# Copying 96 rows of the last batch from HBM to HBM, by index registers on the SyncE queue, with the other stores moved to ScalarE's queue

## The chip, the cores and the metric

One Trainium2 chip, one core. The time is device microseconds of the kernel; medians of a few executions are quoted. Some executions are slow (here: more than 1.5% above the fastest of the same kernel). The medians take them in; a ratio does not: it is the mean time of one kernel's fast runs over that of the other's of the same rounds, so it is not quite the ratio of the quoted medians.

## The reference

```python
def setup_inputs():
    batch, seq, dim = 32, 512, 1024
    return {
        "x": np.random.randn(batch, seq, dim).astype(np.float32),
        "indices": np.random.randint(0, seq, (batch, 128)).astype(np.int32),
    }

def reference(x, indices):
    for b in range(32):
        result[b] = x[b, indices[b]]      # 128 rows of 4 KB for each batch
```

## The kernel before

The first five batches (`HEAD`) are gathered by index into SBUF (the on-chip memory of 128 partitions) and stored. Every other batch has some repeated indices. TensorE and VectorE compute which rows are distinct, GpSimd gathers only those (a slot without a row gets an index out of bounds and is skipped) into one of eight buffers `u`, and a matmul with a 0/1 matrix spreads them to their places; ScalarE copies the result from PSUM (the memory that TensorE writes) and SyncE issues the store. Batch 5 takes part of its rows from two early loads of 128 rows. The slots that stay empty move round all 128 partitions, so that all DMA engines get the same number of rows.

```python
    rank = const.tile([N, 8, 16], I32, name="rank")     # slot number of each partition, for each of 8 groups
    ...
    def store(b):
        if b not in PAIRED:
            nc.sync.dma_start(out=of[b * N:(b + 1) * N], in_=blocks[b])
        elif b % 2:
            nc.sync.dma_start(out=..., in_=blocks[b - 1, "pair"][:])   # two batches in one

    for b in range(HEAD):
        gather(blocks[b], first[:]... if b == 0 else idxT[:, b:b + 1], b)
        store(b)
    ...
    for b in range(HEAD, B):
        spread_rows(b)          # 2 x (matmul, ScalarE copy), then store(b)
        fetch(b + RING)         # the next gather into the buffer that came free
        ...                     # one step of the index work of a later group
```

Of the kernel before, what the change touches and what calls it, by code (L numbers as in the profile page):

```python
# [6 lines left out]
F32 = mybir.dt.float32  # L7
F16 = mybir.dt.float16
I32 = mybir.dt.int32
ALU = mybir.AluOpType  # L10
# [18 lines left out]
def kernel(ctx, tc, x, indices, out):  # L29
# [11 lines left out]



    nc = tc.nc
    B, S, D = x.shape
    N = indices.shape[1]
    HEAD, RING, GROUP, AHEAD, FAR = 5, 8, 3, 4, 1024
    HALF = HEAD
    PAIRED = range(12, 20)
    GROUPS = (B - HEAD) // GROUP  # L50
    assert 2 * N <= S <= FAR and (B - HEAD) % GROUP == 0
    const = ctx.enter_context(tc.tile_pool(name="const", bufs=1))
    ring = ctx.enter_context(tc.tile_pool(name="ring", bufs=1))
    rows = ctx.enter_context(tc.tile_pool(name="rows", bufs=1))
    pick = ctx.enter_context(tc.tile_pool(name="pick", bufs=1))
    junkp = ctx.enter_context(tc.tile_pool(name="junk", bufs=4))
    PS = bass.MemoryType.PSUM
    pbc = ctx.enter_context(tc.tile_pool(name="pbc", bufs=2, space=PS))
    psm = ctx.enter_context(tc.tile_pool(name="psm", bufs=1, space=PS))
    pout = ctx.enter_context(tc.tile_pool(name="pout", bufs=4, space=PS))  # L60
    pe, dve, act = InOrder(tc), InOrder(tc), InOrder(tc)
    mm, v = nc.tensor.matmul, nc.vector
# [4 lines left out]
    vals = const.tile([B, N], indices.dtype, name="vals")  # L67
# [2 lines left out]

    diff = const.tile([N, N], I32, name="diff")
    nc.gpsimd.iota(diff[:], pattern=[[1, N]], base=0, channel_multiplier=-1)
    rank = const.tile([N, 8, 16], I32, name="rank")
    for e in range(8):
        fold = 0
        for bit, col in enumerate((6, 5, 3)):
            fold ^= col * (e >> bit & 1)
        steps = [[(-16 if fold >> bit & 1 else 16) << bit, 2] for bit in (2, 1, 0)]
        nc.gpsimd.iota(rank[:, e], pattern=[[1, 2]] + steps, base=2 * e + 16 * fold, channel_multiplier=0)
    less = const.tile([N, 1], F32, name="less")  # L80
    zero = const.tile([N, 1], F32, name="zero")
    dve(v.memset, zero[:], 0.0)
# [4 lines left out]
    above = const.tile([N, N], F16, name="above")  # L87
    dve(v.tensor_scalar, out=above[:], in0=diff[:], scalar1=0, scalar2=None, op0=ALU.is_gt)
    dve(v.tensor_copy, out=less[:], in_=diff[:, 0:1])
    every = const.tile([N, N], F16, name="every")  # L90
    dve(v.memset, every[:], 1.0)
    turn = const.tile([N, N], F16, name="turn")
    dve(v.tensor_copy, out=turn[:], in_=rank[:].rearrange("p e q -> p (e q)"))
    vf = const.tile([N, N], F16, name="vf")
    dve(v.memset, vf[:], 0.0)
    dve(v.tensor_copy, out=vf[:B],
        in_=vals[:].bitcast(I32).rearrange("p (n two) -> p n two", two=2)[:, :, 0])
# [4 lines left out]
    for k in range(2):  # L102
        load = act(nc.scalar.dma_start, out=early[k][:], in_=xf[HALF * S + k * N:HALF * S + (k + 1) * N])
        if k == 0:
# [7 lines left out]
    idxT = const.tile([N, B], I32, name="idxT")  # L112
# [3 lines left out]
    near = const.tile([N, B], F16, name="near")  # L116
    dve(v.tensor_scalar, out=near[:], in0=tr[:], scalar1=float(-FAR), scalar2=None, op0=ALU.add)

    of = out.flatten_outer_dims()

    def gather(dst, at, b, **kw):
        nc.gpsimd.indirect_dma_start(  # L122
            out=dst, out_offset=None,
            in_=xf[:], in_offset=bass.IndirectOffsetOnAxis(ap=at, axis=0),
            element_offset=b * S * D, **kw)


    blocks = {}
    for b in range(B):
        if b not in PAIRED:  # L130
            blocks[b] = rows.tile([N, D], F32, name=f"block{b}")[:]
# [3 lines left out]
            blocks[b, "pair"] = pair  # L135

    def store(b):
        if b not in PAIRED:
            nc.sync.dma_start(out=of[b * N:(b + 1) * N], in_=blocks[b])
        elif b % 2:  # L140
            nc.sync.dma_start(out=of[(b - 1) * N:(b + 1) * N].rearrange("(t p) d -> p t d", t=2),
                              in_=blocks[b - 1, "pair"][:])

    for b in range(HEAD):
        gather(blocks[b], first[:].bitcast(I32)[:, 0:1] if b == 0 else idxT[:, b:b + 1], b)
        store(b)

    def table(name, dtype):
        return const.tile([N, B], dtype, name=name)

    cnt, lead, slot = table("cnt", F32), table("lead", F16), table("slot", F16)
    nth, at = table("nth", I32), table("at", I32)
    past = const.tile([N, B + 1], F16, name="past")
    dve(v.memset, past[:, HEAD:HEAD + 1], 0.0)
    bcs, packs, spread = {}, {}, {}

    def of_group(g):
        return range(HEAD + g * GROUP, HEAD + (g + 1) * GROUP)

    def cols(t, g):  # L160
        return t[:, HEAD + g * GROUP:HEAD + (g + 1) * GROUP]

    def wide(t):
        return t.rearrange("p (g o) -> p g o", o=1).to_broadcast([N, GROUP, N])

    def step0(g):

# [3 lines left out]
        for k, b in enumerate(of_group(g)):  # L171
            junk = junkp.tile([N, N], F16, name="junk")
            dve(v.scalar_tensor_tensor, out=junk[:], in0=bc[:, k], scalar=idxF[:, b:b + 1], in1=below[:],
                op0=ALU.is_equal, op1=ALU.mult, accum_out=cnt[:, b:b + 1])
        if HALF in of_group(g):
            c = slice(HALF, HALF + 1)
            dve(v.scalar_tensor_tensor, out=cnt[:, c], in0=idxF[:, c], scalar=2.0 * N, in1=cnt[:, c],
# [4 lines left out]

    def step1(g):

        rk = psm.tile([N, GROUP], F32, name="rk")
        pe(mm, rk[:], lhsT=above[:], rhs=cols(lead, g), start=True, stop=False)
        pe(mm, rk[:], lhsT=every[:], rhs=cols(past, g), start=False, stop=True)
        dve(v.tensor_copy, out=cols(nth, g), in_=rk[:])
        dve(v.tensor_scalar, out=cols(nth, g), in0=cols(nth, g), scalar1=N - 1, scalar2=None, op0=ALU.bitwise_and)
        dve(v.scalar_tensor_tensor, out=cols(slot, g), in0=cols(cnt, g), scalar=256.0, in1=cols(nth, g),  # L190
            op0=ALU.mult, op1=ALU.add)
        packs[g] = pack = junkp.tile([N, GROUP, N], F16, name="pack")
        dve(v.tensor_tensor, out=pack[:], in0=turn[:].rearrange("p (o n) -> p o n", o=1).to_broadcast([N, GROUP, N]),
            in1=wide(cols(slot, g)), op=ALU.is_equal)

    def step2(g):

        pos = psm.tile([N, GROUP], F32, name="pos")
        for k, b in enumerate(of_group(g)):
            pe(mm, pos[:, k:k + 1], lhsT=packs[g][:, k], rhs=near[:, b:b + 1], start=True, stop=True)  # L200
        dve(v.tensor_scalar, out=cols(at, g), in0=pos[:], scalar1=float(FAR), scalar2=None, op0=ALU.add)
        s = pick.tile([N, GROUP, N], F32, name=f"s{g}")
        dve(v.tensor_tensor, out=s[:], in0=bcs[g][:, :GROUP], in1=wide(cols(at, g)), op=ALU.is_equal)
        for k, b in enumerate(of_group(g)):
            spread[b] = s[:, k]

    def fetch(b):
        if HEAD <= b < B:
            gather(held[(b - HEAD) % RING][:], at[:, b:b + 1], b, bounds_check=S - 1, oob_is_err=False)

    held = []
# [5 lines left out]
    def half_spread():  # L217

        same = pick.tile([N, 2, N], F32, name="same")
        for k in range(2):  # L220
            dve(v.tensor_scalar, out=same[:, k], in0=bcs[0][:, HALF - HEAD], scalar1=less[:], scalar2=float(k * N),
                op0=ALU.add, op1=ALU.is_equal)
        spread[HALF, "early"] = [same[:, k] for k in range(2)]

    def half_rows(h, last):
        w = slice(h * 512, (h + 1) * 512)
        if not last:
            spread[HALF, h] = pout.tile([N, 512], F32, name="ps")
        ps = spread[HALF, h]
        if last:  # L230
            pe(mm, ps[:], lhsT=spread[HALF], rhs=held[(HALF - HEAD) % RING][:, w], start=False, stop=True)
        else:
            for k in range(2):
                pe(mm, ps[:], lhsT=spread[HALF, "early"][k], rhs=early[k][:, w], start=k == 0, stop=False)
        if last:
            nc.scalar.copy(out=blocks[HALF][:, w], in_=ps[:])  # L236

    def spread_rows(b):
        for h in range(2):
            if b == HALF:  # L240
                half_rows(h, True)
                continue
            w = slice(h * 512, (h + 1) * 512)
            ps = pout.tile([N, 512], F32, name="ps")
            pe(mm, ps[:], lhsT=spread[b], rhs=held[(b - HEAD) % RING][:, w], start=True, stop=True)
            nc.scalar.copy(out=blocks[b][:, w], in_=ps[:])  # L246
        store(b)

    step0(0)
    step0(1)  # L250
    for g in range(AHEAD):
        step1(g)
        if 0 < g < AHEAD - 1:
            step0(g + 1)
        step2(g)
        for b in of_group(g):
            if b < HEAD + RING:
                fetch(b)
        if g == 0:
            half_spread()  # L260
        elif g < 3:
            half_rows(g - 1, False)
    for b in range(HEAD, B):
        spread_rows(b)
        fetch(b + RING)
        g, step = divmod(b - HEAD, GROUP)
        if g + AHEAD < GROUPS:
            (step0, step1, step2)[step](g + AHEAD)
# [30 lines left out]
```

## Time and profile before

| | before |
|---|---|
| time, median of 4 | 88.56 us (87.42 to 88.88) |
| span of the profiled run | 85.4 us |
| DMA | 32.91 MB, 406 GB/s of HBM traffic over the span |
| busy: TensorE, ScalarE, GpSimd, VectorE | 72%, 48%, 40%, 37% |

The span is what the profiler saw from the first to the last instruction; the time of the same execution is 1.8 us longer (87.19 us). The DMA row of the page (busy tenths of the 16 engines, in 40 slices) is the row to read here: it is full from start to end. The prediction below shows these lines and reads them.

### The profile page before, as it was taken

What the parts mean: (1) busy time and instruction counts of PE and PEld (TensorE: products, weight loads), DVE (VectorE), ACT (ScalarE), POOL (GpSimd) and SP (SyncE); (2) the same over time, 40 slices, a digit from 0 to 9 for tenths busy, and PEclk for the clock granted to TensorE, in tenths of its full rate; (3) what the DMA queues carried; (4) which work ended last, traced back from release to release, by engine and by line L of the source; (5) the groups of instructions that cost most, each with busy time, mean ns of one, the idle gap of its engine ahead of it and who ended that gap; (6) DMA issues with size and microseconds to landing.
All of it is one profiled execution on the core that took longest, in us unless ns stands there. A gap on an engine that the chain in (4) does not pass through costs nothing.

```text
span 85.4 us, 829 instructions
## 1 busy us (share of the span) xinstructions
PE 61.1 (72%) x189; PEld 25.5 (30%) x189; DVE 31.7 (37%) x160; ACT 40.6 (48%) x63; POOL 33.9 (40%) x45
## 2 busy tenths in 40 slices
PE   0310379460999999999999999997879988884000
PEld 0300142220434444354444444442212333320000
DVE  3698892864318547375485473000000000000000
ACT  0999920000145566656655666675553454445000
POOL 7687777837024554444555544466000000000000
PEclk9999999999569999999999999999999999999655
DMA  0999999999999999999999999999999999999990
GB/s 1 319 401 263 259 405 413 417 413 426 416 416 424 411 420 420 413 428 418 411 424 416 411 418 418 416 424 418 413 424 418 413 428 413 418 424 418 414 372 23
DMA packets 9636, 32.91 MB, mean 385 GB/s; under 512 B 1584, under 2 KB 1616, under 8 KB 9632
## 3 DMA queue, kind: packets, MB, share of 16 engines
q1 hardware_dynamic: 4736, 16.81, 48.3%
q0 software_dynamic: 4608, 15.01, 45.0%
q10 hardware_dynamic: 288, 1.05, 3.4%
q8 instruction: 1, 0.02, 0.1%
q14 instruction: 3, 0.02, 0.1%
HBM read 17.86 MB, written 16.78 MB: 406 GB/s over the span
## 4 chain that ended last, share of the span: by engine, by line
PE 39%; DMA 21%; DVE 11%; issue 8%; POOL 7%; another core or an unknown queue 2%; ACT 1%; POOLq 1%; SPq 0%; DVEq 0%
PE ps L24 36%; DMA u<-in_x_dram,at 20%; POOL u L122 7%; DVE junk L24 3%; DMA vals<-in_indices_dram 2%; DVE past L24 2%; PE bc L24 2%; DVE pack L24 1%; DVE s L24 1%; DVE nth L24 1%; PE pos L24 1%; DVE lead L24 1%; ACT block L246 1%; DVE same L24 1%
## 5 line engine op out<-in xcount | busy, mean ns | idle before, releaser
L24 PE MATMUL ps<-u,s 128*128 128x512 f32 x108 | 52.8, 624 | 3.4 <-DMA u<-in_x_dram,at 3.4
L122 POOL DMA_INDIRECT u<-in_x_dram,at x27 | 26.9, 998 | 23.8 <-PE ps L24 7.2
L246 ACT COPY block<-ps 128x512 f32<-128x512 f32 x36 | 21.1, 586 | 16.5 <-PE ps L24 15.4
L24 PEld LDWEIGHTS ps<-u,s 128*128 128x128 f32 x108 | 18.9, 193 | 24.7 <-issue 13.4
L246 ACT COPY pair<-ps 128x512 f32<-128x512 f32 x16 | 9.4, 586 | 5.8 <-PE ps L24 4.2
L24 DVE SCALAR_TENSOR_TENSOR junk<-bc,idxF,below 128x128 f16<-128x128 f32 x27 | 8.0, 347 | 7.9 <-PE bc L24 7.9
L24 ACT COPY u<-zero 128x1024 f32<-128x1024 f32 x8 | 7.7, 1040 | 0.0
L236 ACT COPY block<-ps 128x512 f32<-128x512 f32 x2 | 1.2, 586 | 13.2 <-PE ps L24 13.2
L24 PE MATMUL pos<-near,pack 128*128 128x1 f16 x27 | 2.0, 167 | 7.4 <-DVE nth L24 2.9
L24 PE MATMUL ps<-early,same 128*128 128x512 f32 x8 | 5.7, 855 | 0.0
L24 DVE TENSOR_TENSOR pack<-turn,slot 128x384 f16<-128x384 f16 x9 | 5.0, 558 | 0.3
L24 DVE TENSOR_TENSOR s<-bc,at 128x384 f32<-128x384 f32 x9 | 5.0, 557 | 0.3
L24 PEld LDWEIGHTS <-pack 128*128 128x128 f16 x27 | 1.7, 99 | 11.2 <-DVE pack L24 4.3
L24 DVE TENSOR_TENSOR past<-past,lead 128x1 f16<-128x1 f16 x27 | 4.4, 163 | 0.9
L122 POOL DMA_INDIRECT block<-in_x_dram,idxT x4 | 4.1, 1036 | 1.2 <-issue 0.9
L24 PE MATMUL bc<-vf,ident 128*128 128x128 f16 x27 | 3.5, 257 | 1.3 <-DVE same L24 1.3
L24 PEld LDWEIGHTS <-ident 128*128 128x128 f16 x27 | 2.5, 114 | 4.9 <-issue 4.9
L24 DVE TENSOR_SCALAR at<-pos 128x3 int32<-128x3 f32 x9 | 1.4, 160 | 4.2 <-PE pos L24 3.5
L24 DVE CAST nth<-rk 128x3 int32<-128x3 f32 x9 | 1.4, 159 | 4.0 <-PE rk L24 1.9
L21 PE MATMUL pos<-ident,vf 128*128 128x32 f16 x1 | 0.2, 208 | 3.2 <-DVE vf L24 3.2
L24 PE MATMUL rk<-lead,above 128*128 128x3 f16 x9 | 1.6, 172 | 1.1 <-DVE lead L24 1.1
L24 ACT ACT_TABLE_LOAD x1 | 1.3, 1283 | 2.2 <-DVE ident L24 2.2
(31 smaller groups left out, 18.4 us busy)
## 6 DMA issues: line engine op xcount, KB each, us to landing
out_dram<-block SPq DMA_DIRECT2D x24, 512.0 KB
out_dram<-pair SPq DMA_DIRECT2D x4, 1024.0 KB
early<-in_x_dram ACTq DMA_DIRECT2D x2, 512.0 KB
u<-in_x_dram,at POOLq DMA_INDIRECT x27
block<-in_x_dram,idxT POOLq DMA_INDIRECT x4
vals<-in_indices_dram SPq DMA_DIRECT2D x1, 32.0 KB
first<-in_indices_dram SPq DMA_DIRECT2D x1, 1.0 KB
block<-in_x_dram,first POOLq DMA_INDIRECT x1
```

What stands on the lines that cost most here:

```text
L21: self.last = do(*args, **kw)
L24: self.last = do(*args, **kw)
L122: nc.gpsimd.indirect_dma_start(out=dst, out_offset=None, in_=xf[:], in_offset=bass.IndirectOffsetOnAxis(ap=at, axis=0), element_offset=b * ...
L236: nc.scalar.copy(out=blocks[HALF][:, w], in_=ps[:])
L246: nc.scalar.copy(out=blocks[b][:, w], in_=ps[:])
```

## The change

The intent is to save DMA work. A row that goes through SBUF passes the DMA engines twice (gather and store); a row that is copied from HBM to HBM passes once. So 96 of the 128 rows of batch 31 are copied directly. A direct copy takes its row number from a register, eight of which are loaded at a time from an SBUF table, and is cut so that two DMA engines share it. To keep the engines level, five slots of the gather are left empty in most batches, and 123 go round instead of 128. SyncE now issues the row copies, three after each batch, and ScalarE the stores of the spread batches.

The diff, cut to its core (the arithmetic of the slots has more lines):

```diff
+    LONE = B - 1
+    BEGIN = 32
+    MAIN = N - 5
-    rank = const.tile([N, 8, 16], I32, name="rank")     (eight iotas)
+    rank = const.tile([N, 2, 64], I32, name="rank")
+    nc.gpsimd.iota(rank[:], pattern=[[56, 2], [2, 8], [1, 2], [14, 4]], base=-2, channel_multiplier=0)
+    nc.gpsimd.iota(rank[:, :, :8], pattern=[[8, 2], [1, 2], [2, 4]], base=112, channel_multiplier=0)
...
     def store(b):
+        queue = nc.sync.dma_start if b < HEAD else nc.scalar.dma_start
...
+    def halves(row):
+        return row.rearrange("o (a b d) -> (o b) a d", a=2, b=2)
+    def go_alone():
+        for n in range(BEGIN, N, LOAD):
+            loads += nc.values_load_multi_w_load_instructions(flat[LONE:LONE + 1, n:n + LOAD], engines=[SP], ...)[1]
+            for row in loads:
+                nc.sync.dma_start(out=halves(out[LONE, n:n + 1]), in_=halves(x[LONE][bass.ds(row, 1)]))
+                yield
...
+    gather(blocks[LONE][:BEGIN], idxT[:BEGIN, LONE:LONE + 1], LONE)
+    nc.sync.dma_start(out=of[LONE * N:LONE * N + BEGIN], in_=blocks[LONE][:BEGIN])
+    rows_alone(18)
...
         store(b)
+        rows_alone(3)
```

## The prediction

> **What bounds the kernel now.** I read the page's slices of the span first.
>
> ```profile
> span 85.4 us, 829 instructions
> PE   0310379460999999999999999997879988884000
> DMA  0999999999999999999999999999999999999990
> GB/s 1 319 401 263 259 405 413 417 413 426 416 416 424 411 420 420 413 428 418 411 424 416 411 418 418 416 424 418 413 424 418 413 428 413 418 424 418 414 372 23
> DMA packets 9636, 32.91 MB, mean 385 GB/s; under 512 B 1584, under 2 KB 1616, under 8 KB 9632
> ```
>
> The 16 DMA engines are busy in every slice but the first and the last, while TensorE starts late and ends early. Packets under 8 KB less those under 2 KB are 9632 - 1616 = 8016 rows of 4 KB: 4096 stored, 256 of the early load, and 3664 gathered (640 for the first five batches, 3024 for the other 27, whose repeated indices are skipped). The table of stretches shows how firm this bound is.
>
> ```profile
> 5.00:10.00 5.00, 0.62 (x7) 0.34 (x7) 4.29 (x23) 5.00 (x6) 3.62 (x5) 1.00 0.99 300
> 30.00:40.00 10.00, 10.00 (x35) 4.37 (x34) 5.96 (x30) 6.34 (x11) 5.13 (x6) 1.00 1.03 419
> 70.00:75.00 5.00, 4.21 (x10) 1.35 (x8) 0.00 (x0) 2.65 (x5) 0.00 (x0) 1.00 1.03 419
> 80.00:85.40 5.40, 0.00 (x0) 0.00 (x0) 0.00 (x0) 0.00 (x0) 0.00 (x0) 0.50 0.59 242
> ```
>
> The last columns are DMA share and GB/s. From 15 to 80 us the rate stays near 419, so one engine moves 26.2 GB/s, and a row of 4096 bytes costs 156 ns of one engine. 8016 rows / 16 engines = 501 rows, 78.2 us: nearly the span. The end of the chain of waits says the same: a transfer, the last matmuls and copies, and then the stores still queued.
>
> ```profile
> 58.96 16.67 DMA u<-in_x_dram,at
> 75.77 1.97 PE ps L24 x4
> 77.76 0.59 ACT block L246
> ```
>
> So compute matters only where it leaves DMA without work, and a DMA that can be issued only after the others are done adds its full time. For the cost of issuing I read the tile view of the output, and what SyncE waits for.
>
> ```profile
> L139 SPq DMA_DIRECT2D out_dram<-block x24: 332/332/360, 7.2 to 78.4; - x24
> L141 SPq DMA_DIRECT2D out_dram<-pair x4: 372/374/387, 40.9 to 52.3; - x4
> SPq L139 <- ACT block L246: 30.1, 18, 2.1
> ```
>
> One issue takes 0.33 to 0.37 us of the sequencer; today SyncE has only 30 and waits for ScalarE's copies.
>
> **What the Trainium skill says.** All from its page "DMA: Bandwidth & Descriptors".
> - "Why a DMA increments its semaphore by 16 and not by 1": the slowest dimension of the access patterns sets how many engines take part, and from SyncE and ScalarE these are the lowest-numbered. An outer dimension of two means engines 0 and 1. The trace before has no such DMA and cannot confirm it.
> - "The descriptor swizzle": in a transfer of 128 partitions, partitions 64 to 71 belong to engines 8 and 9. The new ranks leave just partitions 66, 67 and 69 to 71 mostly empty. If that table holds for the indirect gather, the wrong pair is relieved. The profile has no engine numbers, so this is open.
> - "Latency and other measured facts": a register load (tensor_load) costs at least some 600 ns. The trace before has none.
> - [...]the index load issues at 1.19 us and its data is used at 2.94, in the timeline.
>
> **The change, part by part.**
>
> *DMA volume.* Batch 31 was gathered (113 distinct rows) and stored (128): 241 row passes. Now 32 + 32 pass through SBUF and 96 go from HBM to HBM once: 160. Saved 81 passes / 16 x 156 ns = 0.8 us, if all engines stay equal. This is the whole intended gain, 0.9%.
>
> *Balance.* The 96 rows are 48 on each of two engines, 48 x 156 ns = 7.5 us if a 1 KB piece costs a quarter of a row. I worked the slots out from the fixed draw: two engines get 144 and 120 gathered rows over the 26 spread batches, the others about 188. If those two are the ones that copy, they carry 192 and 168 and all is level. If they are not, each copying engine carries 48 rows too many.
>
> *Head.* In the order of the built program the second small iota now stands behind the first gather on GpSimd, and the cast of the rank table, which needs it, stands in VectorE's fixed order ahead of the indices' transpose. Before:
>
> ```profile
> 2.34 0.23 DVE L24 CAST turn<-rank 128x128 f16<-128x128 int32 x1 [0.59 <-POOL rank L79]
> 2.76 1.12 POOL L122 DMA_INDIRECT block<-in_x_dram,first  x1 [0.45 <-DMA first<-in_indices_dram]
> 4.18 0.95 POOL L122 DMA_INDIRECT block<-in_x_dram,idxT  x1 [0.30 <-DVE past L24]
> ```
>
> The cast moves from 2.34 to about 4.2 us (gather ends at 3.88, then an iota of about 0.2). Cast, vf, transpose, idxT took about 1.0 us of work, so the second gather goes at 5.3 instead of 4.18: 1.1 us later. DMA is not at full rate there anyway (300 GB/s from 5 to 10 us), and the first store fills some of the hole; I book 0.5 us.
>
> *VectorE and TensorE.* Four more small VectorE operations per group, 4 x 9 x 0.17 = 6 us on an engine busy 37%, and nine more tiny matmuls: beside DMA, nothing.
>
> *Stores on ScalarE.* 22 issues of about 0.35 us, some 8 us beside its 40.6 busy: hidden by itself. But DMA completions of SyncE and ScalarE share eight semaphores in rotation, and each DMA waits until the last user of its semaphore is done. Reading semaphore numbers and wait values in the built program, some stores now wait for the store two batches back (blocks 7, 8, 11, 24, 25), where eight could be out before. That may leave some holes; I book 1 us.
>
> *The row copies at the end: the part that decides.* The same listing shows SyncE's rows falling behind. In the semaphores' order the store of batch 30, the last, comes ahead of row copy 74 (counting from 0), and that copy waits for it. SyncE issues in order, so row copies 74 to 95, 22 of 96, cannot start before the last big store has landed. They then run with nothing beside them: 22 x (0.33 us issue + about 0.12 for the address arithmetic in registers and the wait, my estimate) = 9.9 us, and the two register loads in that stretch (eight indices each) at 0.6 to 1.6 us, say 1.1, give 2.2. Sum 12.1 us, paced by SyncE, not by the two engines: one row is two 1 KB pieces each, about 80 ns.
>
> *Sum.* DMA now ends about 84.2 us into the span. The last store: 84.2 - 0.8 + 0.5 (head) + 1.0 (waits) = 84.9 if the relieved engines are the right ones. If not, engines 0 and 1 carry 37 of the 74 copied rows without relief, 37 - 5 saved = 32 rows x 156 ns = 5 us later than before, about 89.5. I can't tell which and take 87. Plus 0.5 for the semaphore to reach SyncE, 12.1 for the tail, 1.5 for the last copy to land, 1.2 from last packet to span end: 102.3. The measured median is about 2 to 3 us over the span (88.36 against 85.4), which would give 104.8. I shade it to 102, because a DMA to two engines may issue faster than one to sixteen.
>
> **The rivals.**
> 1. *All hidden, small gain.* Row copies run beside the big transfers, SyncE is ahead, engines level: 0.8 us less, minus the head, 87.5 to 88.5. For it: the care in the slot numbers, and SyncE's idleness now. Against it: the wait of row copy 74 on the last store, a wait on a constant that cannot be overtaken.
> 2. *Wrong engines, no tail.* The waits cost little but engines 0 and 1 carry 48 extra rows: 7.5 us less some 1 us saved, about 94 to 95. For it: the swizzle in the skill; against: someone chose partitions 64 to 71 and five slots, presumably with a reason.
> 3. *SyncE slower than I think.* If register addresses make an issue 0.8 us, the tail is 22 x 0.8 + 3 = 21 us, and the time 108 to 112. Nothing in the trace before speaks to it.
> 4. *Throttled stores.* ScalarE stuck behind semaphores holds PSUM and so TensorE: DMA share falls under 0.9 in the middle, 3 to 5 us on top of any of these.
>
> **Range and chances.** The tail is certain by the order of the program, and even at 0.33 us a row with 0.6 us loads it is 8.5 us: with the last store at 81 at best, 81 + 8.5 + 3 + 2 = 94.5. The bottom of the range, 93, is a little under that; the top, 111, is the slow issue with the wrong engines in part. Faster by 2% would need under 86.6, more than the full saving: 3%. Within 2%: 6%, if I misread the semaphores. Slower: 91%.
>
> **What would show it.** Right: the DMA row of the page falls to about one tenth in the last five or six slices, with a few tens of GB/s; the chain of waits ends in SyncE issues of the row copies; the last ScalarE copy is some 15 us before the end. The second gather starts near 5.3 us. The 0.45 us step between row copies is read from SyncE's timeline near the end. Engines level: the DMA share stays 1.0 until the last store; wrong pair: a shelf at two tenths of activity ahead of the tail. Wrong: row copies finished while stores still run, and full DMA up to the end.

## The result, and the profile after

The changed kernel takes 129.07 us (127.71 to 129.41, 4 runs). The ratio to before is 1.466, 95% interval 1.443 to 1.488: far slower, and 18 us above the top of the range.

The page of the kernel after, by slices:

```profile
span 127.2 us, 1164 instructions
PE   0212756698989729999956679595000000000000
ACT  1996000155336043465304163643400000000000
DMA  2989999999999999979999997474552000000000
GB/s 29 344 276 280 392 384 416 415 414 412 398 411 406 420 388 401 350 202 415 342 407 410 403 396 307 199 321 171 215 207 88 5 3 5 4 5 5 4 4 4
```

A slice is 3.18 us here. The kernel has three stretches: DMA nearly full to slice 24 (76 us), though with holes that the kernel before has not; half full to slice 30 (97 us); and a tail of nine slices with 3 to 5 GB/s. The table of stretches (columns as in the prediction: last are DMA share and GB/s) gives the last two in numbers:

```profile
70.00:80.00 10.00, 7.76 (x16) 2.71 (x16) 0.00 (x0) 3.75 (x8) 0.09 (x1) 1.00 0.87 352
80.00:90.00 10.00, 6.54 (x14) 2.49 (x14) 0.00 (x0) 4.30 (x8) 0.00 (x0) 1.00 0.54 218
90.00:100.00 10.00, 0.00 (x0) 0.00 (x0) 0.00 (x0) 1.58 (x3) 0.00 (x0) 0.50 0.41 162
100.00:110.00 10.00, 0.00 (x0) 0.00 (x0) 0.00 (x0) 0.00 (x0) 0.00 (x0) 0.50 0.02 5
```

(The lower mean clock of this run, 0.83, comes mostly from the tail: it reads 0.50 from 90 us on, where TensorE has nothing to do. It does not set the end, which is SyncE's.)

What runs in the tail, from SyncE's timeline near the end (start, length, what), and what one such issue costs, from the tile view of the output and the view of the line that loads the registers (min/median/max in ns, first and last start):

```profile
95.60 29.29 SPq L165 DMA_DIRECT2D out_dram<-in_x_dram  x31
```

```profile
L165 SPq DMA_DIRECT2D out_dram<-in_x_dram x96: 7/632/978, 9.7 to 124.3; - x96
L146 ACTq DMA_DIRECT2D out_dram<-block x18: 338/339/353, 26.2 to 93.9; - x18
L148 ACTq DMA_DIRECT2D out_dram<-pair x4: 378/383/389, 47.7 to 66.6; - x4
```

```profile
L159 SPq TENSOR_LOAD <-flat x12: 15/1058/2494, 8.7 to 117.1; - x12
```

The issue of a row copy takes 0.63 us where the issue of a store of 128 rows takes 0.34. With the address arithmetic, a register move and the gaps between them the step from one row copy to the next is 0.84 us, and each group of eight adds a load of 1.06 us. Thus 96 x 0.84 + 12 x 1.06 = 93 us: SyncE alone, never waiting, needs more than the whole span of before, and its first copy goes out at 9.7 us. In the tail it does not wait for anything: 31 copies in 29.29 us, with three loads between them, and 31 x 0.84 + 3 x 1.06 is 29.2. Earlier it does wait, for stores; from its list of waits (us in total, times, longest):

```profile
SPq L165 <- DMA out_dram<-block: 7.0, 2, 5.4
SPq L165 <- DMA out_dram<-pair: 4.2, 3, 2.5
```

That is 11.2 us more on SyncE.

The last store is issued at 93.9 us, where before it was at 78.4. What held it is in the list of waits of ScalarE (us in total, times, longest):

```profile
ACT block L295 <- DMA out_dram<-in_x_dram: 13.8, 6, 4.6
ACT block L295 <- DMA out_dram<-block: 6.4, 3, 2.7
ACT pair L295 <- DMA out_dram<-block: 5.8, 1, 5.8
```

26 us of waits for DMAs. In the kernel before ScalarE never waits for a DMA, as it issues no stores. A semaphore is a counter that a DMA raises when its data has landed. The DMAs of SyncE and ScalarE take their completion semaphores in turn from the same eight, and each is issued only when the previous user of its semaphore is done. In the built program's listing the store of batch 30, for instance, comes after row copy 61 on its semaphore, that one after the store of batch 25 (in the trace they go out in this order, at 93.9, 91.0 and 81.4 us). So stores wait for row copies that SyncE has not reached yet, and ScalarE stops copying. TensorE's weight loads then wait 21.8 us for ScalarE's copies (11.2 before), and GpSimd's gathers 11.7 us for TensorE (7.2 before).

The head came as predicted. From the timeline of the kernel after:

```profile
3.94 0.19 POOL L82 IOTA rank<- 128x16 int32 x1
4.16 0.23 DVE L24 CAST turn<-rank 128x128 f16<-128x128 int32 x1 [2.14 <-POOL rank L82]
5.47 0.95 POOL L128 DMA_INDIRECT block<-in_x_dram,idxT  x1 [1.35 <-DVE idxF L24]
```

The second gather starts at 5.47 us; it was 4.18.

### The profile page after: what moved, and what is told of

Same layout as the page of the kernel before. It is cut to its first block, busy times and chain, and to the rows that moved or that the text cites. A ratio compares the mean times of both kernels' runs of the same rounds, so it can differ in the third digit from the quotient of the medians.

```text
span 127.2 us, 1164 instructions
## 1 busy us (share of the span) xinstructions
PE 61.9 (49%) x192; PEld 24.8 (20%) x192; DVE 36.5 (29%) x194; ACT 37.5 (29%) x61; POOL 33.2 (26%) x39
## 3 DMA queue, kind: packets, MB, share of 16 engines
q1 hardware_dynamic: 1536, 3.18, 6.8%
## 4 chain that ended last, share of the span: by engine, by line
DMA 28%; SPq 11%; PE 10%; issue 9%; DVE 8%; ACT 3%; ACTq 1%; POOL 1%
DMA out_dram<-pair 13%; PE ps L24 8%; SPq L165 7%; DMA out_dram<-in_x_dram 7%; DMA out_dram<-block 6%; SPq L159 4%; ACT block L295 2%; DVE turns L24 2%; DVE nth L24 2%; DMA first<-in_indices_dram 1%; ACTq L146 1%; DVE junk L24 1%; ACT pair L295 1%; PE pos L24 1%; DVE pack L24 1%
## 5 line engine op out<-in xcount | busy, mean ns | idle before, releaser
L128 POOL DMA_INDIRECT u<-in_x_dram,at x26 | 26.3, 1013 | 32.4 <-PE ps L24 11.7
L295 ACT COPY block<-ps 128x512 f32<-128x512 f32 x34 | 18.3, 588 | 25.6 <-DMA out_dram<-in_x_dram 13.8
L295 ACT COPY pair<-ps 128x512 f32<-128x512 f32 x16 | 9.1, 589 | 12.6 <-DMA out_dram<-block 5.8
L128 POOL DMA_INDIRECT block<-in_x_dram,idxT x5 | 4.6, 924 | 2.6 <-DVE idxF L24 1.3
L285 ACT COPY block<-ps 128x512 f32<-128x512 f32 x2 | 1.2, 586 | 13.5 <-issue 13.5
L24 DVE TENSOR_TENSOR pack<-turn,slot 128x384 f16<-128x384 f16 (+1 forms) x9 | 4.9, 544 | 0.3
L24 DVE TENSOR_TENSOR s<-bc,at 128x384 f32<-128x384 f32 (+1 forms) x9 | 4.9, 543 | 0.3
L24 PEld LDWEIGHTS <-above 128*128 128x128 f16 x18 | 1.9, 111 | 6.4 <-issue 6.4
L24 DVE TENSOR_SCALAR turns<-rk 128x3 f32<-128x3 f32 (+1 forms) x9 | 1.4, 159 | 3.7 <-PE rk L24 3.6
L24 PE MATMUL rk<-lead,above 128*128 128x3 f16 (+1 forms) x18 | 1.8, 169 | 1.0 <-DVE cnt L24 1.0
L24 PEld LDWEIGHTS ps<-early,same 128*128 128x128 f32 x8 | 1.9, 257 | 1.5 <-issue 1.5
```

Of the source, the lines that this page charges most:

```text
L24: self.last = do(*args, **kw)
L128: nc.gpsimd.indirect_dma_start(out=dst, out_offset=None, in_=xf[:], in_offset=bass.IndirectOffsetOnAxis(ap=at, axis=0), element_offset=b * ...
L285: nc.scalar.copy(out=blocks[HALF][:, w], in_=ps[:])
L295: nc.scalar.copy(out=blocks[b][:, w], in_=ps[:])
```

## The experiments

The theories that the runs were to tell apart: A, SyncE's issue of the row copies is simply too long for one queue; B, row copies and stores wait for each other through the shared semaphores; C, the wrong pair of DMA engines was relieved; D, the stores cost where they are now. Kernels with a wrong result by intent are marked.

**1. No row copies.** The whole of batch 31 is gathered and stored early; everything else stays.

```diff
-    BEGIN = 32
-    MAIN = N - 5
+    BEGIN = N
+    MAIN = N
-    alone = go_alone()
+    alone = iter(())
```

> Theory A (SyncE's issue of 96 row copies, about 0.84 us each plus 1.05 us per load of eight indices, is the longest queue) and theory B (row copies and big stores wait for each other through eight shared semaphores) both say that without row copies the kernel is bound by its DMA volume again: 88 to 90 us, a little over the kernel before for the later second gather. A rival D, that the stores on the ScalarE queue cost by themselves, would leave it at 93 us or more.

89.96 us, ratio 1.019 (1.012 to 1.027). So the row copies bring nearly all of the loss. (Its result was wrong: with an even number of slots in rotation the rounding points, by my reading of the formula, one row in 256 at a slot that does not exist. Run 8 uses 127 slots and is correct.)

**2. Half of the row copies.**

```diff
-    BEGIN = 32
-    MAIN = N - 5
+    BEGIN = 80
+    MAIN = N - 2
```

> 48 row copies. Theory A: SyncE needs 8.3 + 48 x 0.84 + 6 x 1.1 + 2.5, plus some waits, about 60 to 65 us, and is done before the stores are: 88 to 91 us. Theory B alone: stores still stand behind row copies up to the middle, so 95 us or more. Theory C (the wrong pair of DMA engines is relieved): about 2.5 us on top of A, 91 to 93.

92.54 us, correct, ratio 1.049 (1.042 to 1.056). The last row copy is issued at 74 us, so SyncE is not the end here, and still 3% are lost against run 1. ScalarE waits 11.5 us in four waits for row copies. Halving the rows takes away 37 of the 41 us, far more than half: above some number of rows SyncE's queue outlasts the stores, and below it the rest is left: the waits, the head (run 8) and perhaps the wrong pair. The time lies in the range that the expectation gave for theory C; this run does not part it from the waits.

**3. Fixed addresses (wrong result).** The source row is a constant; no loads, no address arithmetic.

```diff
-            loads += nc.values_load_multi_w_load_instructions(...)[1]
+            loads = [None] * LOAD
...
-                nc.sync.dma_start(out=halves(out[LONE, n:n + 1]), in_=halves(x[LONE][bass.ds(row, 1)]))
+                nc.sync.dma_start(out=halves(out[LONE, n:n + 1]), in_=halves(x[LONE, n:n + 1]))
```

> Wrong result on purpose: the 96 rows are copied from fixed addresses, without loads of indices and address arithmetic. Theory A with the register address as the cost: an issue falls from 0.63 us to 0.33 to 0.40 us, a row from 0.84 to about 0.45, SyncE is done by about 60 us, and the time is 88 to 95 (the top if theory C holds too). If a small DMA on two engines costs 0.63 us whatever its address, SyncE needs 8 + 96 x 0.7 = 75 us and the time is 90 to 105.

101.91 us (2 runs), ratio 1.158 (1.149 to 1.168). The tile view of the output in this run, and below that in run 4:

```profile
L163 SPq DMA_DIRECT2D out_dram<-in_x_dram x96: 606/626/1457, 1.7 to 94.5; - x96
```

The issue still takes 0.63 us: the register is not what makes it dear. It costs the rest of the step (0.84 against 0.68 us) and the loads. As the first copies go out at 1.7 us instead of 9.7, and 96 x 0.68 are 65 us, this kernel shows what remains when SyncE's work is shorter than the span: it still loses 14 us. Two things are seen in its trace. ScalarE waits 21.1 us for row copies and stores before its copies, and between 90 and 94 us the DMA share is 0.37. And the early loads, now behind row copies, go out at 4.6 and 8.7 us (1.7 and 2.1 in the change), so that the second slice has 27 GB/s where the change has 344. How the 14 us divide, between these and the wrong pair (run 9), was not tested.

**4. Fixed addresses, 16 engines (wrong result).** As run 3, each row in 16 pieces of 256 bytes.

```diff
-        return row.rearrange("o (a b d) -> (o b) a d", a=2, b=2)
+        return row.rearrange("o (b d) -> (o b) d", b=16)
```

> Wrong result on purpose: e_fixed_rows with each row in 16 pieces of 256 bytes on 16 engines instead of four of 1 KB on two. If the 0.63 us of an issue come from using fewer than 16 engines, the issue falls to 0.33 to 0.40 us. If they come from the HBM to HBM form, it stays near 0.63 us. The time: relief no longer fits, but no engine is overloaded: 90 to 102, the top if the issue stays.

```profile
L163 SPq DMA_DIRECT2D out_dram<-in_x_dram x96: 509/587/1723, 1.6 to 85.4; - x96
```

Issue 0.59 us: nor is it the number of engines. The DMAs from HBM to HBM in these runs, of 2 or 16 engines, with registers or without, took 0.59 to 0.64 us to issue in the median (the one long copy of run 7: 0.78). Those between HBM and SBUF from SyncE and ScalarE took 0.33 to 0.46 in the median, but for SyncE's first five stores in run 4 (0.52); single ones go up to 1.1. Why is open. The time, 111.05 us (2 runs, the profiled one slow; the fast one 109.92), fell outside what I expected; the scheduler had put 20 of the copies ahead of the first store, and I did not follow it further.

**5. Stores on the GpSimd queue.** Its semaphores are others, so after row copy 17 no row copy waits for a store and no store for a row copy.

```diff
-        queue = nc.sync.dma_start if b < HEAD else nc.scalar.dma_start
+        queue = nc.sync.dma_start if b < HEAD else nc.gpsimd.dma_start
```

> The stores of the spread batches go on the GpSimd queue, which has semaphores of its own, so that after the first row copies SyncE waits for no store and no store for SyncE. Theory A alone: SyncE runs through at 0.84 us a row and 1.05 us a load, 8.3 + 97 + 2.4 + 2.2 = 110 us of span, 112 us. Theory B alone: 90 to 95. If both hold, as I think, 110 to 113: some 17 us of the 40 are the mutual waits.

117.44 us (2 runs: 116.12, and 118.77), correct. ScalarE no longer waits for any DMA, and SyncE's row copies wait 0.7 us for stores. The page of this run, the fast one:

```profile
span 114.4 us, 1164 instructions
DMA  1979999999999999999999999999981000000000
GB/s 26 350 258 318 360 368 401 404 409 400 407 390 370 341 384 416 413 413 411 421 412 414 416 403 407 406 418 410 397 335 70 27 5 5 3 4 4 4 4 3
```

DMA is full up to 85 us, as before the change, and then SyncE issues its last 29 row copies alone. Without the mutual waits SyncE paces the end, some 3 us above the 110 to 113 that I expected; the waits account for the other 129.07 - 116.12 = 12.9 us, fast run against fast runs. That fits the 11.2 us that SyncE waited for stores in the change. Slices 30 and 31 (70 and 27 GB/s) are a shelf, which is run 9's subject.

**6. Stores back on SyncE.** Only that part of the change undone.

```diff
-        queue = nc.sync.dma_start if b < HEAD else nc.scalar.dma_start
+        queue = nc.sync.dma_start
```

> The change with that part alone undone which moved the stores to ScalarE: all 26 batches' stores on SyncE again, between the row copies. Theory A: SyncE gets 22 issues of 0.36 us more and still paces the end, 129 + 8 = 137 us; with stores waiting in line behind row copies perhaps 140. If instead the stores on ScalarE, stuck behind semaphores, were what made the change slow (theory B alone): 105 to 115.

129.93 us (2 runs), correct, ratio 1.475 (1.457 to 1.493): the same as the change. Moving the stores to ScalarE neither caused the loss nor prevented it; theory D falls. ScalarE waits for no DMA then. The expectation's 137 us left out that SyncE's own waits shrink too: its list has 3.3 us for stores (2.3 before row copies, 1.0 before stores) where the change has 11.2. These 7.9 us less make up for the some 8 us of issue that 22 more stores cost.

**7. One long copy in place of 96 (wrong result): failed.** In three kernels (`e_block_64`, `e_block_0`, `e_block_none`) the 96 rows were copied unshuffled by a single DMA on the same two engines, to test theory C without the issues. The scheduler put the stores of the first five batches behind those of later ones on the shared semaphores, and the first of them went out at 55 us instead of 8. The times (95.84, 97.50, 95.87 us) tell nothing of the engines. They show once more what a shared semaphore does: SyncE's first stores wait 63.1 us in sum for paired stores of ScalarE. (The expectation for `e_chunk_64` below says that they waited for the long copy; in the trace that copy's last packet ends at 27.8 us.) What was expected of the first:

> Wrong result on purpose: the 96 rows are copied from HBM to HBM unshuffled, by one DMA on the same two engines in the same 1 KB pieces, so the volume and the relief of partitions 64 to 71 stay and the 96 issues go. If the relieved pair is the pair that copies: 0.8 us under e_no_rows (89.96), 89 us. If it is not (theory C): the copying engines carry 545 row times where all carried 501, 44 x 156 ns = 6.9 us over e_no_rows, about 97, with some two engines busy for the last 6 us.

**8. The cast later, no row copies.** As run 1 with 127 slots, and the cast of the rank table behind the transpose.

```diff
-    turn = const.tile([N, N], F16, name="turn")
-    dve(v.tensor_copy, out=turn[:], in_=rank[:]...)
...
     dve(v.tensor_copy, out=flat[:], in_=vals[:]...)
+    turn = const.tile([N, N], F16, name="turn")
+    dve(v.tensor_copy, out=turn[:], in_=rank[:]...)
```

> No row copies, and the cast of the rank table moved behind the transpose of the indices, so that the second gather no longer waits for the second iota. If the 2.0 us that e_no_rows lies over the kernel before are this wait in the head: 88 to 88.5. If they are the stores on ScalarE or the longer VectorE chain: still 89.5 to 90.

```profile
4.27 0.28 DVE L24 CAST turn<-rank 128x128 f16<-128x128 int32 x1
4.30 0.95 POOL L128 DMA_INDIRECT block<-in_x_dram,idxT  x1 [0.23 <-DVE idxF L24]
```

The second gather is back at 4.30 us, and the time is 88.38 us, ratio 1.006 (1.002 to 1.010), correct. The order in the head costs 1.3% of 88 = 1.1 us. For the longer VectorE chain and the stores on ScalarE together some 0.6% remain (0.2 to 1.0%).

**9. Twelve copies of 8 rows (wrong result): which engines copy.** The head of run 8; the 96 rows unshuffled in twelve DMAs on the same two engines in the same 1 KB pieces, each after the copies of every second batch. Three kernels differ in the slots left empty: five of the partitions 64 to 71 as in the change, five of the partitions 0 to 7, or (nearly) none.

```diff
+    def chunk(k, after):
+        rows = slice(BEGIN + k * CHUNK, BEGIN + (k + 1) * CHUNK)
+        part = lambda t: t[LONE, rows].rearrange("n (a b d) -> b (n a) d", a=2, b=2)
+        copy = nc.sync.dma_start(out=part(out), in_=part(x))     # after the ScalarE copy `after`
...  e_chunk_0 alone:
-    nc.gpsimd.iota(rank[:, :, :8], pattern=[[8, 2], [1, 2], [2, 4]], base=112, channel_multiplier=0)
+    nc.gpsimd.iota(rank[:, :, :8], pattern=[[-8, 2], [1, 2], [2, 4]], base=120, channel_multiplier=0)
...  e_chunk_none alone:
-    MAIN = N - 5
+    MAIN = N - 1
```

> Wrong result on purpose, and e_block_64 put right: there the first stores waited for the long copy through a shared semaphore, which spoilt it. Now the 96 rows go unshuffled in 12 DMAs of 8 rows on the same two engines, each after the copies of every second batch, on the head of e_turn_later (88.38). A 1 KB piece takes 46 ns, so a copying engine gets 192 x 46 ns = 8.8 us. Right pair relieved: engines of 308 + 144 rows and 8.8 us against 501 rows before, 78.9 against 77.7 us of work: 88 to 89.5. Wrong pair (theory C): 308 + 189 rows and 8.8 us, 8.2 us over e_turn_later: 96 to 97, with two engines alone for the last 6 to 8 us.

> As e_chunk_64 with partitions 0 to 7 left empty instead of 64 to 71. Theory C with engines 0 and 1 serving partitions 0 to 7[...]: 88 to 89.5. If the author's 64 to 71 were right: 96 to 97. If neither pair is the copying one: both 96 to 97.

> As e_chunk_64 with no engine relieved. Under each mapping the copying engines get 308 + 183 rows and 8.8 us: 7.2 us over e_turn_later, about 95.5.

| slots left empty | time | ratio to before |
|---|---|---|
| partitions 64 to 71 | 95.87 us | 1.079 (1.070 to 1.087) |
| partitions 0 to 7 | 90.13 us | 1.011 (1.006 to 1.017) |
| none | 95.40 us | 1.079 (1.073 to 1.085) |

The stretches at the end, of `e_chunk_64` and then of `e_chunk_0` (whose profiled run was slow, 91.3 us; its fast runs are 89.1 to 90.1 us):

```profile
86.00:88.00 2.00, 0.00 (x0) 0.00 (x0) 0.00 (x0) 0.00 (x0) 0.00 (x0) 0.54 0.13 52
88.00:90.00 2.00, 0.00 (x0) 0.00 (x0) 0.00 (x0) 0.00 (x0) 0.00 (x0) 0.50 0.13 52
90.00:92.00 2.00, 0.00 (x0) 0.00 (x0) 0.00 (x0) 0.00 (x0) 0.00 (x0) 0.50 0.13 49
```

```profile
84.00:86.00 2.00, 0.00 (x0) 0.00 (x0) 0.00 (x0) 0.00 (x0) 0.00 (x0) 0.50 0.92 375
86.00:88.00 2.00, 0.00 (x0) 0.00 (x0) 0.00 (x0) 0.00 (x0) 0.00 (x0) 0.50 0.19 73
```

A share of 0.13 is 2 engines of 16, at 26 GB/s each: for 6 us the two copying engines work alone. With slots in partitions 0 to 7 empty the shelf is gone but for 2 us at a share of 0.19. The change relieves the wrong pair, and relieving it is worth no more than relieving none. In the change itself this is hidden, as SyncE ends much later; run 5's shelf shows it there.

`e_chunk_0` is also the change as it was meant, with issues that cost next to nothing and the right engines. It is not faster than the kernel before, nor than run 8 (1.011 against 1.006). The packet records give the reason for a part: a 1 KB piece takes 46 ns of an engine and a row of 4 KB 159, so a row copied in four pieces costs 184 ns. Of the 81 x 156 ns = 12.6 us of engine time that were to be saved, 96 x 25 ns = 2.4 us go. In 86 to 88 us the last chunk's pieces still run.

**10. The repairs in a correct kernel.** Half of the rows, partitions 0 to 7 empty, the cast later; and the same with the stores on GpSimd's queue.

```diff
-    BEGIN = 32
-    MAIN = N - 5
+    BEGIN = 80
+    MAIN = N - 2
-    ... pattern=[[8, 2], [1, 2], [2, 4]], base=112 ...
+    ... pattern=[[-8, 2], [1, 2], [2, 4]], base=120 ...
     (the cast as in run 8; for e_half_0_pool the queue as in run 5)
```

> A correct result with 48 row copies and two of the found causes repaired: the slots left empty lie in partitions 0 to 7 (one per copying engine), and the rank cast stands behind the transpose. From e_half_rows (92.5): 1.6 us for the head, and the copying engines get 308 + 162 rows and 96 x 46 ns = 4.4 us, 77.3 us of work, where they had 80.8: 88 to 89.5. If the mutual waits are what e_half_rows lost, it stays at 90.5 or more.

> As e_half_0, with the stores of spread batches on the GpSimd queue, whose semaphores no row copy shares. If waits between rows and stores still cost there: 1 to 2 us under e_half_0, 87.5 to 88.5. If not, the same as e_half_0, or slower where GpSimd's stores delay its gathers.

`e_half_0`: 91.83 us (90.34 to 93.41; the fast runs 91.40 and 90.34), ratio 1.031 (1.013 to 1.050). `e_half_0_pool`: 91.57 us, ratio 1.038 (1.030 to 1.047). Both missed what I hoped for. From the waits and the stretches of `e_half_0`, and from the stretches of `e_half_0_pool`:

```profile
ACT block L295 <- DMA out_dram<-in_x_dram: 8.7, 2, 4.6
```

```profile
80.00:86.00 6.00, 6.00 (x16) 2.65 (x15) 0.00 (x0) 4.09 (x8) 0.00 (x0) 1.00 0.69 282
```

```profile
70.00:80.00 10.00, 7.82 (x16) 2.71 (x16) 0.00 (x0) 4.69 (x8) 3.41 (x8) 1.00 1.03 419
86.00:90.00 4.00, 0.00 (x0) 0.00 (x0) 0.00 (x0) 0.00 (x0) 0.00 (x0) 0.50 0.01 3
```

With the stores on ScalarE the waits for row copies put TensorE behind; at 80 to 86 us it is busy all the time (6.00 of 6.00) and DMA has too little to do (0.69). These are theory B's waits in a correct kernel, as the expectation's second half said. `e_half_rows` shows the same: 11.5 us of such waits, and a DMA share of 0.86 from 80 to 86 us. With the stores on GpSimd no hole is left until the queue runs out, and the last packet ends at 86.6 us. Then 3.4 us pass until the program ends, which in the kernel before are 1.2. The trace shows where 1.7 of them lie (closing instructions of the program, line L344):

```profile
L344 POOLq DRAIN  x3: 46/107/9235, 80.0 to 89.7; - x3
```

SyncE is through with its closing waits at 87.6 us; GpSimd's first DRAIN of the close, of 9.2 us, ends at 89.2, and only then does the rest go on. In the kernel before it had ended at 77.0, long before SyncE. So what the waits cost was in part exchanged for a later close; this is read from one trace, and no run takes the close away. No version with row copies beat the kernel before.

## Why the prediction was wrong

The direction (slower, at 0.91) and the place (a tail of row copies on SyncE with DMA at next to nothing) were right. The size was off: 102 us against 129.07, and in span 102.3 against 127.2, of which the tail is 15 us and the last store 9.5. The tail takes nine slices where I named five or six. By its own terms:

- **The cost of a row copy: the step that failed.** I took "0.33 us issue + about 0.12", from stores between SBUF and HBM, for a kind of DMA that the trace before did not have. It is 0.84 us, of which 0.63 is the issue. The register load I put at 1.1; it took 1.06. The tail came to 29 x 0.84 + 3 x 1.06 = 27.5 us (97.3 to 124.9), where I had 12.1. My hope that a DMA to two engines issues faster, for which I shaded the sum, was wrong in sign. Rival 3 had the size of the step (0.8 us) but put it down to the register; run 3 shows that the register costs only 0.16 us of it, besides the loads.
- **What the tail waits for.** I let row copy 74 wait for the last store. In the trace it is issued at 104.3 us, some 8 us after that store has landed. SyncE was late already, with 29 rows left and not 22, by its own issues and by 11.2 us of waits for earlier stores. The wait of row copy 74 was in the program, but it was not the last to end. I looked for the binding wait and did not add up the queue: 96 x 0.84 + 12 x 1.06 is 93 us. Even with my own 0.45 the sum of what SyncE has to do would have been the first number to write down.
- **The last store, 87 against 96.5 us landed.** I booked 1 us for throttled stores and gave 3 to 5 in rival 4. It is the second error, of 9.5 us: ScalarE waits 26 us in sum, because the row copies that its stores wait for are late themselves. I read the two errors as one, a SyncE twice as slow as assumed making the waits longer as well; no run shows the waits with a fast issue alone. Run 5 takes the waits away and gains 12.9 us; the other 28 us over the kernel before stay.
- **The engines.** I left it open between two cases 5 us apart. Runs of part 9 settle it: the pair is wrong, 95.87 against 90.13 us. What the Trainium skill says in "DMA: Bandwidth & Descriptors", sections "The descriptor swizzle" (partitions 0 to 7 belong to engines 0 and 1) and "Why a DMA increments its semaphore by 16 and not by 1" (a copy over two engines from SyncE takes the two lowest), fits these runs, with an indirect gather too. I gave a stranger's care with slot numbers as much weight. In the change's own time it does not show.
- **The head.** Second gather at 5.3 predicted, 5.47 measured; 0.5 us booked, 1.1 measured (runs 1 and 8).
- **VectorE, TensorE and the stores on ScalarE:** nothing predicted by themselves beside the waits, and no more than some 0.6% found (run 8).
- **Time and span.** I added 2 to 3 us to the span, from a median and the span of another execution. The same execution took 1.8 us more.
- **The saving.** 0.8 us predicted at best; I took a 1 KB piece at a quarter of a row, 39 ns; it takes 46. With few issues and the right engines no gain could be measured (`e_chunk_0`).

Shown by runs: the row copies are the cause (1), through SyncE's issue and the mutual waits (5); the wrong pair (9); the head (8). Open: why a DMA from HBM to HBM takes 0.6 us to issue, how the loss of run 3 divides, the time of run 4, and what is left of the loss in `e_half_0_pool` beside its late close.

## What to carry to other kernels

Before a transfer is cut into many small ones, multiply their number by the step of the queue that issues them and set it against the span; a saving of 0.8 us of DMA time cannot pay for 93 us of a sequencer. Measure the step on the very form of DMA, with one look, as an issue of another form may cost half. And look up which semaphores the queues share: a slow queue holds up a fast one through them, even where no data connects the two.

## What the Trainium skill lacked or had wrong

- "DMA: Bandwidth & Descriptors" does not give the issue time on this chip by form. Here a DMA from HBM to HBM took 0.59 to 0.64 us of SyncE in the median (2 or 16 engines, fixed or register address), a store from SBUF 0.33 to 0.37 us in the kernel before.
- The same page, section "Latency and other measured facts", gives a floor of some 600 ns for a register load, and no time for eight registers from SBUF at once. That took 1.06 us in the median of twelve, 2.49 us at most.
- The same page, section "The descriptor swizzle", is written for a plain transfer of 128 partitions. For the partitions tried here it fits an indirect gather too: the two engines of a two-engine copy are those of partitions 0 to 7 and not of 64 to 71 (90.13 us with slots of the former left empty, 95.87 with the latter).
- No page has a measured time of one small piece from HBM to HBM on an engine: 46 ns for 1 KB here, 159 ns for a row of 4 KB.
- No page that I found warns that completion semaphores shared by two queues couple them: 26 us of waits on ScalarE in the change, none with the stores on another queue.
